# First projections of a hybrid attention and retention layer: Strassen's seven products of halves, in two passes over the input

## Chip, cores and metric

One NeuronCore of a Trainium2 chip runs the whole layer. The metric is the device time of one execution in microseconds (us), the lower the better. All data is float32. TensorE multiplies in the float32r form, and the kernel splits each operand into a high part (rounded to float32r) and a low part (what is left), so that one product is three matmuls: high x high, high x low, low x high.

## What is computed

The layer has 4096 tokens of width 1024. Cut to what matters here:

```
h = rms_norm(x, norm_gain)                  # x * rsqrt(mean(x*x) + 1e-6) * gain
proj = h @ w_in                             # 1024 -> 3584 columns
qa, ka, va, ga, qr, kr, vr, gr = split(proj, 512, 512, 512, 512, 256, 256, 512, 512)
attn = dilated_attention(rope(qa), rope(ka), va)       # 8 heads x 64, three (window, dilation) branches
ret  = retention(rotate(qr), rotate(kr), vr)           # 4 heads, keys 64, values 128
mixed = concat(silu(ga) * attn, silu(gr) * ret * ret_gain)
out = rms_norm(x + mixed @ w_out, final_gain)
```

The first stage of the kernel, `phase1`, computes five of these projections: qa and ka (1024 columns), the retention's qr and kr (512 together), and the attention's va (512). It rotates q, k and r by position and stores all of them in DRAM.

## The kernel before

There are three stages. `phase1` makes the first projections. `phase2` runs the attention heads, with the retention between their pieces as filler. `phase3` computes the gates and the output projection. In every stage the program order of each engine's instructions is written out by hand (`manual_schedule` with `ORDERED`: TensorE, ScalarE = ACT, VectorE = DVE, GpSimd = POOL, SyncE = SP). An engine takes its instructions in that order, so one that waits holds up all behind it on its engine.

`phase1` before the change goes through 8 blocks of 512 tokens. The input comes transposed, with channels on the partitions: 8 tiles of 128 channels x 512 tokens per block. `make_h` (L163 to L175) treats each tile: ACT squares it (L168) and rounds the high part (L169), DVE subtracts for the low part (L170), and POOL adds the square to a running sum (L172). The tile that takes the square has one buffer, so the next square waits for that addition. The RMS scale comes at the end of a block: `root` sums over partitions on TensorE (L188), takes the power -0.5 on POOL (L199) and builds a diagonal (L201); `along_free` turns it into a row over tokens (L209, L211). The cosine and sine tables are multiplied by that row on POOL (`scaled`, L217), so q, k and r are scaled while they are rotated.

A block has 12 weight-stationary banks (four each of q, k, r; weights 128 x 128 stationary, 512 tokens moving) and four banks of v, in which 128 tokens are stationary and 512 weight columns move. Each bank takes 8 channel tiles x 3 matmuls, so a block is 16 x 24 = 384 matmuls of 512 columns. `rotate` (L235 to L260) reads two finished PSUM banks A and B: four multiplications by tables with an operand in PSUM (L240 to L243), a subtraction and an addition (L244, L245). For q and k, ACT rounds the high part (L252 for q; L257 for k, in a permuted order) and DVE subtracts (L253, L258); SP issues the stores (L259, for r L248). `store_values` scales v on ACT (L273) and issues six stores per 128 tokens from ACT's own queue (L275, L278, L282).

All weights stay in SBUF: they are loaded and split at the start (`Split.split`, L83 and L84). After the last block the second stage begins with values of the retention, chunk by chunk (`filler`; matmuls L48 to L50 on `V`); the chunks' inputs are split in `split_h_chunk` (L432, L435).

Of the kernel before, what the change touches and what calls it, by code (L numbers as in the profile page):

```python
# [24 lines left out]
S = 4096  # L25
D = 1024
# [87 lines left out]

def phase1(tc, io, dr, right, ahead):
# [5 lines left out]
    with ExitStack() as ctx:  # L121
        wp = ctx.enter_context(tc.tile_pool(name="p1w", bufs=1))
        hp = ctx.enter_context(tc.tile_pool(name="p1h", bufs=9))
        xp = ctx.enter_context(tc.tile_pool(name="p1x", bufs=4))
        sm = ctx.enter_context(tc.tile_pool(name="p1s", bufs=2))
        tp = ctx.enter_context(tc.tile_pool(name="p1t", bufs=1))
        op = ctx.enter_context(tc.tile_pool(name="p1o", bufs=2))
        pmm = ctx.enter_context(tc.tile_pool(name="p1mm", bufs=7, space=PSUM))
        pss = ctx.enter_context(tc.tile_pool(name="p1ss", bufs=1, space=PSUM))
        ctx.enter_context(tc.manual_schedule(engines=ORDERED))  # L130

# [6 lines left out]
        qgain = wp.tile([128, KT], F32, name="qgain1")  # L138
        nc.vector.tensor_scalar(qgain, gain, -0.125, None, ALU.mult)

        W = {}
        qp = ahead["qp"] = {0: right.open("p2q")}
        wpool = ahead["wpool"] = right.open("p12w")
        for g in ("r", "k", "q", "v"):
            p = {"v": wp, "q": wpool}.get(g) or right.open(f"p1w{g}")
            i = "qkrv".index(g)
            W[g] = Split(
                nc,
                p,
                f"w1{g}",  # L150
                io["w1"][:, i * 512 : (i + 1) * 512],
                scale=qgain if g == "q" else gain,
                tag="w" if g == "q" else None,
                room=[(qp[0], "q00"), (qp[0], "q10")] if g == "r" else None,
            )

        def load_xt(b, k):
            x = xp.tile([128, BLK], F32, tag="x", name="xt1")
            nc.sync.dma_start(x, io["xT"][k * 128 : (k + 1) * 128, b * BLK : (b + 1) * BLK])
            return x  # L160
# [3 lines left out]
        def make_h(b, k, raw):  # L164

            h = hp.tile([128, 2, BLK], F32R, tag="h", name="h1")
            sq = tp.tile([128, BLK], F32, tag="sq" if k else "acc", name="sq1")
            nc.scalar.activation(sq, raw, AF.Square)  # L168
            nc.scalar.activation(h[:, 0, :], raw, AF.Copy)  # L169
            nc.vector.tensor_tensor(h[:, 1, :], raw, h[:, 0, :].bitcast(F32), ALU.subtract)  # L170
            if k:
                nc.gpsimd.tensor_tensor(sums[b], sums[b], sq, ALU.add)  # L172
            else:
                sums[b] = sq
            return h  # L175

        def load_tables(b, n):
            tab = tp.tile([128, 2, BLK], F32, tag=f"tab{n}", name=f"tab{n}1")
            for i, nm in enumerate((f"cos{n}", f"sin{n}")):
                nc.sync.dma_start(tab[:, i, :], io[nm][:, b * BLK : (b + 1) * BLK].unsqueeze(0).broadcast_to([4, 32, BLK]))  # L180
            return tab
# [33 lines left out]
        def scaled(tab, rb):  # L215
            for i in range(2):
                nc.gpsimd.tensor_tensor(tab[:, i, :], tab[:, i, :], rb, ALU.mult)  # L217

        def products(g, i, hs, p, ks=range(KT)):

            for k in ks:
                mm3(
                    nc,
                    p,
                    [(*W[g].at(k, slice(i * 128, i * 128 + 128)), hs[k][:, 0, :], hs[k][:, 1, :])],
                    k == 0,
                    k == KT - 1,
                )

        def bank():  # L230
            return pmm.tile([128, BLK], F32, tag="mm", name="mm1")

        def rotate(b, kind, idx, A, B, tab):
            cols = slice(b * BLK, (b + 1) * BLK)
            cos, sin = tab[:, 0, :], tab[:, 1, :]  # L235
# [3 lines left out]
            t4 = tp.tile([128, BLK], F32, tag="u", name="t4_1")  # L239
            nc.vector.tensor_tensor(o1, A, cos, ALU.mult)  # L240
            nc.vector.tensor_tensor(t4, A, sin, ALU.mult)
            nc.vector.tensor_tensor(t2, B, sin, ALU.mult)
            nc.vector.tensor_tensor(o2, B, cos, ALU.mult)  # L243
            nc.vector.tensor_tensor(o1, o1, t2, ALU.subtract)  # L244
            nc.vector.tensor_tensor(o2, o2, t4, ALU.add)  # L245
            for part, o in enumerate((o1, o2)):
                if kind == "r":
                    nc.sync.dma_start(dr["r"][idx, :, part, :, cols], o)  # L248
                    continue
                hl = op.tile([128, 2, BLK], F32R, tag="hl", name="hl1")  # L250
                if kind == "q":
                    nc.scalar.activation(hl[:, 0, :], o, AF.Copy)  # L252
# [10 lines left out]
        def values(b, i, k, hs, p):  # L263
            cs = slice(i * 128, (i + 1) * 128)
            mm3(nc, p, [(hs[k][:, 0, cs], hs[k][:, 1, cs], *W["v"].at(k, slice(0, 512)))], k == 0, k == KT - 1)

# [27 lines left out]
        for _ in range(4):  # L294
            load_first()
        for k in range(KT):
            W["q"].split(k)
            hcur.append(make_h(0, k, xts[k]))
            if len(xts) < KT:
                load_first()  # L300
# [1161 lines left out]
```

## Time and profile before

| | |
|---|---|
| median of 3 runs | 2414.75 us (2413.61 to 2418.51) |
| the profiled execution | 2416.7 us, span 2414.9 us |
| mean granted clock of TensorE | 0.988 |
| busy: TensorE (PE) | 2342.5 us, 97% |
| busy: its weight loads (PEld) | 1986.1 us, 82% |
| busy: DVE, ACT, POOL | 1485.8, 990.0, 725.0 us |
| DMA | 362.59 MB, mean 150 GB/s |

How to read the lines below. The page's busy list has, for each engine, the busy time, its share of the span and the count of instructions. A window line has, for a stretch of time in us, its length, then busy time and count for PE, PEld, DVE, ACT and POOL (or for the one engine asked for), then the mean granted clock of TensorE (1.00 is full), the busy share of the DMA engines, and GB/s. A timeline line has start, duration, engine, source line, operation, output <- inputs, shape, count, and in brackets the idle time before it and what ended it. A group line has the same for all instructions of a line and form: busy us and mean ns of one, then the idle time before them with its releasers. A busy PE is not PE at its peak, since the ends of matmuls are modelled: the distance between starts, or the count in a window, gives the rate.

### The profile page before, as it was taken

To read this page: it belongs to the slowest core of one execution; us is meant where nothing else is said; L and a number is where in the kernel's file an instruction comes from. 1 tells how busy PE (TensorE), PEld (TensorE's weight loads), DVE (VectorE), ACT (ScalarE), POOL (GpSimd) and SP (SyncE) were. 2 spreads that over 40 slices of the span, in tenths; PEclk is the share of its full clock that TensorE was granted. 3 is DMA by queue.
4 is the path that set the end of the run, shared out by engine and by line. 5 is a ranking of instruction groups with operands and counts; after the bars stand their busy time and mean duration, and the time that the engine had idled before them with its cause. 6 is when DMAs were issued, how large, how long until landed. Compare 5 with 4: busy or idle time off the path is not lost. (4 is left out here: it accounts for less than half of the span.)

```text
span 2414.9 us, 41800 instructions
## 1 busy us (share of the span) xinstructions
PE 2342.5 (97%) x14568; PEld 1986.1 (82%) x14568; DVE 1485.8 (62%) x3923; ACT 990.0 (41%) x2865; POOL 725.0 (30%) x765
## 2 busy tenths in 40 slices
PE   7999999999997999999999999998899999999998
PEld 5778888888885888888888887877789899999997
DVE  5643543543534878787887879786665565665654
ACT  4322222222211666666666666667222222222221
POOL 5312112112112535353544535455221121121110
PEclk9999999999998999999999999999999999999999
DMA  6343343343356766758586765746575656656553
GB/s 192 130 145 107 133 144 107 133 144 111 129 147 202 165 163 139 181 131 189 131 180 148 169 156 131 176 125 196 143 182 154 145 171 152 145 168 154 142 153 92
DMA packets 404259, 362.59 MB, mean 150 GB/s; under 512 B 191848, under 2 KB 334824, under 8 KB 398928
## 3 DMA queue, kind: packets, MB, share of 16 engines
q1 hardware_dynamic: 389408, 332.91, 52.6%
q10 hardware_dynamic: 14112, 25.43, 3.4%
q8 instruction: 115, 1.88, 0.3%
q0 software_dynamic: 528, 1.58, 0.2%
q14 instruction: 96, 0.79, 0.1%
HBM read 241.18 MB, written 118.64 MB: 149 GB/s over the span
## 5 line engine op out<-in xcount | busy, mean ns | idle before, releaser
L688 DVE CUSTOM_DVE_ANT_0 S<-S,mask 128x256 f32<-128x256 f32 (+1 forms) x768 | 308.4, 402 | 156.7 <-PE S L667 123.5
L695 ACT ACTIVATE P<-S,nm 128x256 f32<-128x256 f32 (+1 forms) x768 | 337.2, 449 | 46.9 <-DVE nm L688 43.9
L50 PE MATMUL g<-h,wg 128*128 128x256 f32 x1024 | 290.6, 284 | 0.0
L704 PE MATMUL T<-ident,P 128*128 128x128 f32 x1368 | 213.3, 274 | 0.0
L49 PE MATMUL po<-wo,m 128*128 128x512 f32 x512 | 200.6, 392 | 0.0
L50 PEld LDWEIGHTS g<-h,wg 128*128 128x128 f32 x1024 | 197.1, 192 | 0.0
L737 PE MATMUL O<-pt,v 128*64 128x128 f32 (+1 forms) x1968 | 195.8, 325 | 0.0
L667 PE MATMUL S<-kk,qc 128*128 128x256 f32 x1024 | 186.9, 306 | 6.8 <-issue 2.8
L48 PE MATMUL po<-wohi,m 128*128 128x512 f32 x448 | 178.9, 399 | 6.9 <-ACT m L40 5.4
L1251 POOL TENSOR_TENSOR rs<-v,mhalf 128x1 f32<-128x1 f32 x32 | 17.5, 547 | 547.0 <-DVE v L1249 384.9
L667 PEld LDWEIGHTS S<-kk,qc 128*128 128x128 f32 x1024 | 150.0, 191 | 34.7 <-issue 17.5
L50 PE MATMUL po<-wohi,m 128*128 128x512 f32 x448 | 176.9, 396 | 0.2 <-DVE m L41 0.2
L172 POOL TENSOR_TENSOR sq<-sq,sq 128x512 f32<-128x512 f32 x56 | 76.3, 1362 | 331.4 <-ACT sq L168 331.4
L435 POOL TENSOR_TENSOR hc<-hr,hc 128x512 fp32r<-128x512 f32 x64 | 85.9, 1343 | 289.3 <-ACT hc L434 149.6
L737 PEld LDWEIGHTS O<-pt,v 128*64 128x64 f32 x1968 | 121.2, 137 | 60.3 <-issue 31.2
L704 PEld LDWEIGHTS T<-ident,P 128*128 128x128 f32 x1368 | 163.8, 141 | 0.2 <-ACT wg0hi L87 0.2
L695 ACT ACTIVATION_READ_ACCUMULATOR P<-S,nm 128x1 f32 x768 | 157.5, 205 | 0.0
L48 PE MATMUL g<-h,wg1hi 128*128 128x256 f32 x512 | 145.9, 286 | 4.6 <-ACT e L1190 4.5
L40 ACT ACTIVATE m<-e 128x256 fp32r<-128x256 f32 x128 | 53.1, 417 | 234.5 <-DVE e L1197 137.8
L49 PE MATMUL g<-h,wg1hi 128*128 128x256 f32 x512 | 146.9, 287 | 0.9 <-DVE h L483 0.7
L48 PE MATMUL g<-h,wg0hi 128*128 128x256 f32 x512 | 144.8, 283 | 1.8 <-ACT e L1190 1.8
L49 PE MATMUL g<-h,wg0hi 128*128 128x256 f32 x512 | 144.9, 283 | 0.0
(212 smaller groups left out, 6120.7 us busy)
## 6 DMA issues: line engine op xcount, KB each, us to landing
q<-dr_q SPq DMA_DIRECT2D x128, 256.0 KB
hr<-in_xT_dram SPq DMA_DIRECT2D x64, 512.0 KB
wb<-dr_w SPq DMA_DIRECT2D x128, 192.0 KB
o<-dr_o SPq DMA_DIRECT2D x192, 128.0 KB
v<-dr_v SPq DMA_DIRECT2D x94, 256.0 KB
xt<-in_xT_dram SPq DMA_DIRECT2D x64, 256.0 KB
dr_q<-hl SPq DMA_DIRECT2D x32, 512.0 KB
dr_k<-hl SPq DMA_DIRECT2D x32, 512.0 KB
```

Source lines behind the costliest of these rows:

```text
L40: nc.scalar.activation(dst[:, 0], src, AF.Copy)
L48: nc.tensor.matmul(out, wh, xh, start=first and i == 0, stop=False)
L49: nc.tensor.matmul(out, wh, xl, start=False, stop=False)
L50: nc.tensor.matmul(out, wl, xh, start=False, stop=last and i == n - 1)
L172: nc.gpsimd.tensor_tensor(sums[b], sums[b], sq, ALU.add)
L435: nc.gpsimd.tensor_tensor(hc[:, :, 1, :], src, hc[:, :, 0, :].bitcast(F32), ALU.subtract)
L667: nc.tensor.matmul(s[:, j * 256 : (j + 1) * 256], qq[h, t, half][:, off : off + 128] if br == 0 else it["q"][:, t, i, :], rhs, start=(j == ...
L688: nc.vector.tensor_tensor_reduce(sv, sv, mask[:, it["br"], c0:256], 1.0, BIG, ALU.add, ALU.min, accum_out=nm[:, col : col + 1])
L695: nc.scalar.activation(it["P", i // 2][:, i % 2, c0:256], sv, AF.Exp, bias=nm[:, col : col + 1], scale=-1.0, accum_out=den[:, col : col + 1])
L704: nc.tensor.transpose(t[:, j * 128 : (j + 1) * 128], it["P", bank][:, j // 2, j % 2 * 128 : j % 2 * 128 + 128], ident)
L737: nc.tensor.matmul(o[64 * bank : 64 * bank + 64, c0 : c0 + 128 * m], vt[h, br, idx // 8][:, idx % 8, :], it["pt"][:, a : a + m, :].rearran ...
L1251: nc.gpsimd.tensor_tensor(rs, v, mhalf, ALU.pow)
```

## The change

The multiplication X W is cut into halves in three directions: the 1024 channels (`part` 0 and 1, four tiles each), a block's 512 tokens (`half`, 256 each), and the columns of the weights (two halves). Eight products of halves are replaced by seven (Winograd's form of Strassen's method): `P1`, `P2`, `P6`, `P5`, `P7`, `P3`, `P4`, in this order. P6, P5, P7 and P4 take sums of halves of x (POOL, `sum_t`); P6, P5, P7 and P3 sums or differences of halves of the weights, made once per pass. Results are collected in PSUM banks x, y and z (`SUMS`); copies of unfinished banks are taken by ACT (`snapshot`), and added back by DVE (`join`).

There are two passes over the input. In the first (q = 0 to 7) the weight halves make the attention's q (bank 0) and k (bank 1); in the second (q = 8 to 15) the retention's q and k together (bank 0), and v (bank 1; tokens are stationary there). Each product has one step per bank, so a block of a pass has 14 steps (`STEPS`), each of 24 matmuls of 256 columns. Input is loaded in both passes; the RMS row of the second is read from DRAM. Everything else is put on steps: `at(step, fn)` places work behind that step's matmuls, in the order in which it was entered, first that of an earlier block, then the inputs of the next.

v is now stored from SP's queue. q's factor -0.125 is applied when it is stored. The weights of the second pass are prepared around step 112 into tiles that the first pass leaves (loads of 2 MB, sums on DVE and POOL, splits on ACT with DVE or POOL), and its P4 weights a little later. At the start the loads of weights (128-column pieces, 512 bytes) and of half blocks of x alternate. At the end k, q, the retention's value weights and the first x chunk of the second stage are loaded and split in the last ten steps. The second stage's pools are opened at the beginning. The other stages are unchanged.

The core of the diff, removed lines left out:

```
+PRODUCTS = ("P1", "P2", "P6", "P5", "P7", "P3", "P4")
+SUMS = {"P1": "x", "P2": "y", "P6": "x", "P5": "z", "P7": "x", "P3": "z", "P4": "x"}
+HALF = BLK // 2
+STEPS = 2 * NP
...
+        rawp = pool("p1x", 3)
+        hp = pool("p1h", 3)
+        dp = pool("p1d", 2)
+        tp = pool("p1t", 1)
+        op = pool("p1o", 2)
+        mp = pool("p1m", 7)
+        pyz = pool("p1y", 2, space=PSUM)
+        pss = pool("p1ss", 1, space=PSUM)
+        pz = pool("p1z", 2, space=PSUM)
+        px = pool("p1px", 3, space=PSUM)
...
+        def split_x(q, prod, engine=None, each=False):
+            t = xs[q, prod] = hp.tile([128, 2, 4, HALF], F32R, tag="h", name="h1")
+            src = source(q, prod)
+            for ks in [slice(k, k + 1) for k in range(4)] if each else [slice(0, 4)]:
+                nc.scalar.activation(t[:, 0, ks, :], src[:, ks, :], AF.Copy)
+                (engine or nc.vector).tensor_tensor(t[:, 1, ks, :], src[:, ks, :], f32(t[:, 0, ks, :]), ALU.subtract)
...
+        def square(q, j):
+            sq = tp.tile([128, BLK], F32, tag="sq" if j else "acc", name="sq1")
+            nc.scalar.activation(sq, xraw[q, j // 4][:, j % 4, :], AF.Square)
+            if j:
+                nc.gpsimd.tensor_tensor(sums[q], sums[q], sq, ALU.add)
...
+        def snapshot(q, s, bank, name, half):
+            t = M[q, name, bank] = mp.tile([128, 512], F32, tag="m", name="m1")
+            p = banks[q, s, bank]
...
+                nc.scalar.activation(t, p, AF.Copy)
...
+        def join(q, s, bank, name, half, part):
+            t, p = M[q, name, bank], banks[q, s, bank]
...
+                nc.vector.tensor_tensor(t, p, t, ALU.add)
...
+        def rotate(q, bank, half):
+            if half == 0:
+                A, B = M.pop((q, "m1", bank)), banks.pop((q, "x", bank))
+            else:
+                A, B = M.pop((q, "u2", bank)), M.pop((q, "m5", bank))
...
+            nc.vector.tensor_tensor(two(t2), two(B), sin, ALU.mult)
+            nc.vector.tensor_tensor(two(o2), two(B), cos, ALU.mult)
+            nc.vector.tensor_tensor(two(o1), two(A), cos, ALU.mult)
+            nc.vector.tensor_tensor(two(A), two(A), sin, ALU.mult)
             nc.vector.tensor_tensor(o1, o1, t2, ALU.subtract)
+            nc.vector.tensor_tensor(o2, o2, A, ALU.add)
...
+        def inputs(q):
+            s = STEPS * q
+            at(s - 14, load_x, q, 0)
+            at(s - 8, load_x, q, 1)
+            if q < NBLK:
+                for j in range(4):
+                    at(s - 7 + j, square, q, j)
+                    at(s - 3 + j // 2, square, q, 4 + j)
+            at(s - 4, sum_t, q, 1)
+            at(s - 4, split_x, q, "P1")
+            at(s - 2, split_x, q, "P2")
+            at(s - 2, sum_t, q, 2)
+        for q in range(NB2):
+            s = STEPS * q
+            first, last = q % NBLK == 0, q % NBLK == NBLK - 1
+            if q:
+                inputs(q)
+            at(s, split_x, q, "P6")
+            at(s + 2, split_x, q, "P5", nc.gpsimd)
+            at(s + 3, sum_t, q, 3)
+            at(s + 4, split_x, q, "P7")
+            at(s + 6, split_x, q, "P3", nc.gpsimd if q >= NBLK or last else None)
+            at(s + 7, sum_t, q, 4)
+            at(s + 8, split_x, q, "P4", nc.gpsimd if last else None)
+            if q < NBLK:
+                at(s + (2 if q else 6), make_root, q)
+                at(s + (5 if q else 8), make_rb, q)
+            else:
+                at(s + 5, load_rb, q)
+            at(s + 7, load_tables, q)
+            at(s + 9, scale_tables, q)
+            for bank in range(2):
+                at(s + 1 + 2 * bank, snapshot, q, "x", bank, "m1", 0)
+                at(s + 6 + bank, snapshot, q, "x", bank, "u2", 1)
+                at(s + 8 + bank, snapshot, q, "z", bank, "m5", 1)
+                at(s + 4 + bank, join, q, "y", bank, "m1", 0, 0)
+                at(s + 9 + bank, join, q, "x", bank, "m5", 1, 1)
+                at(s + 11 + bank, join, q, "z", bank, "u2", 1, 0)
+            if q < NBLK:
+                order = ((11, 0, 1), (13, 0, 0), (15, 1, 0), (17, 1, 1))
+            else:
+                order = ((11, 0, 1), (12, 1, 1), (13, 0, 0), (14, 1, 0))
+            for n, bank, half in order:
+                at(s + n, last_sum, q, bank, half)
...
+        for step in range(STEPS * NB2 + 5):
+            q, i = divmod(step, STEPS)
+            prod, bank = PRODUCTS[i // 2] if q < NB2 else None, i % 2
+            if step in start:
+                start[step]()
+            if q < NB2 and step >= 4:
+                product(W[q // NBLK], q, prod, bank, units=(0, 1))
+            for fn, args, kw in todo.pop(step, []):
+                fn(*args, **kw)
```

`last_sum` calls `rotate`, or in the second pass scales and stores v. Each tuple of `order` is a step, a bank and a half: (15, 1, 0) and (17, 1, 1) fall on steps 1 and 3 of the next block.

More of the change, by code (lines that the diff above doesn't have):

```diff
@@ L137, in phase1 @@
         make_identity(nc, ident)
[L138 to L160, printed above, removed]
-        sums = {}
[L164 to L172, printed above, removed]
-            else:
-                sums[b] = sq
-            return h
@@ L213, in along_free @@
             return rb
-        def scaled(tab, rb):
-            for i in range(2):
[L217 to L231, printed above, removed]
@@ new lines, in phase1, with is_v, rcol @@
+        M = {}
+        def is_v(q, bank):
+            return q >= NBLK and bank == 1
+        def rcol(q, half, u):
+            n = 4 * (q % NBLK) + 2 * half + u
+            return rs[:, n : n + 1]
+        def snapshot(q, s, bank, name, half):
+            t = M[q, name, bank] = mp.tile([128, 512], F32, tag="m", name="m1")
+            p = banks[q, s, bank]
+            if is_v(q, bank):
+                for u in range(2):
+                    us = slice(256 * u, 256 * u + 256)
+                    nc.scalar.activation(t[:, us], p[:, us], AF.Copy, scale=rcol(q, half, u))
+            else:
+                nc.scalar.activation(t, p, AF.Copy)
@@ L309, in phase1 @@
-        diag = root(0)
-        for k in range(KT):
-            W["k"].split(k)
-        rb = None
-        def make_room(gi):
-            if gi == 1:
-                ahead["qq"] = {(0, i, 0): load_q(nc, qp, dr, 0, i, 0) for i in range(2)}
-            if gi == 3:
-                ahead["w2"] = Split(nc, wpool, "w2", io["w2"], scale=gain, tag="w")
-                ahead["w2"].load(xp.tile([128, BLK], F32, tag="x", name="raw1"))
-        GROUPS = [("q", 0), ("q", 1), ("k", 0), ("k", 1), ("r", 0), ("r", 1)]
@@ new lines, in phase1, with w2_load, w2_split, first_k @@
+        for i in range(2):
+            for k in (2 * i, 2 * i + 1):
+                at(s + 3 + 2 * i, split_p4, k)
+                at(s + 5 + 2 * i, split_p4_end, k)
+        def w2_load():
+            ahead["w2"] = Split(nc, wpool, "w2", io["w2"], scale=gain, tag="w")
+            ahead["w2"].load(mp.tile([128, 512], F32, tag="m", name="raw1"))
+        def w2_split(ks):
+            for k in ks:
+                ahead["w2"].split(k)
+        def first_k():
+            ahead["kk"] = load_k(nc, kka, dr, 0)
@@ new lines, in phase1 @@
+        for k in range(4):
+            load_x(0, 0, (k, H2))
+            load_w(0, Bb[k], 1, 4 + k)
+            load_w(0, Ba[k], 1, k)
+            load_x(0, 1, (k, H2))
+        for prod, t, part in (("P1", Aa, 0), ("P2", Ab, 1)):
+            h = xs[0, prod] = hp.tile([128, 2, 4, HALF], F32R, tag="h", name="h1")
+            for k in range(4):
+                split_w(0, prod, t, part, ks=[k])
+                src = source(0, prod)[:, k, :]
+                nc.scalar.activation(h[:, 0, k, :], src, AF.Copy)
+                nc.vector.tensor_tensor(h[:, 1, k, :], src, f32(h[:, 0, k, :]), ALU.subtract)
+                for bank in range(2):
+                    product(W[0], 0, prod, bank, [k])
```

444 lines of the change are left out of this document (305 added, 139 removed).

## Prediction

> **What bounds the kernel now.** I read the page first, its busy list and its slices; then the windows of 100 us; then the timeline of single engines in one block of the first stage.
>
> ```profile
> PE 2342.5 (97%) x14568; PEld 1986.1 (82%) x14568; DVE 1485.8 (62%) x3923; ACT 990.0 (41%) x2865; POOL 725.0 (30%) x765
> ```
>
> ```profile
> 0.00:100.00 100.00, 84.38 (x336) 65.41 (x337) 60.25 (x75) 40.76 (x64) 46.04 (x37) 0.97 0.53 170
> 300.00:400.00 100.00, 100.00 (x437) 81.39 (x437) 40.28 (x55) 22.19 (x33) 18.24 (x15) 1.00 0.38 125
> 700.00:800.00 100.00, 82.93 (x400) 68.22 (x400) 49.27 (x103) 22.15 (x46) 23.16 (x28) 0.91 0.68 191
> ```
>
> TensorE is never idle in the middle of the stage: 437 matmuls of 512 columns in 100 us, 0.229 us each, at the full clock, while DVE is busy for 40 of 100 us and POOL for 18. So this stage is bound by TensorE, and matmul columns saved there are time saved, as long as the others keep up. The stage begins and ends less well filled.
>
> **The matmuls.** The timeline of TensorE gives the price of a 256-column product, from the gates of the last stage, and the end of the first stage:
>
> ```profile
> 1903.23 0.28 PE L48 MATMUL g<-h,wg1hi 128*128 128x256 f32 x1
> ...
> 1906.09 0.40 PE L48 MATMUL po<-wohi,m 128*128 128x512 f32 x1
> ```
>
> ```profile
> 756.31 0.39 PE L50 MATMUL mm<-w1vhi,h 128*128 128x512 f32 x1
> ```
>
> Twenty-four 256-column matmuls lie between the first two rows: 2.86 us, 0.119 us each, 4% more per column than at 512. Removed are 8 blocks x 384 = 3072 matmuls of 512 columns (703 us at 0.229). Added are 16 half passes x 14 steps x 24 = 5376 of 256 (641 us); a step is 2.86 us and a block of 14 steps 40.05 us. The matmuls alone give back 62 us. [...]
>
> **What else a block of the first pass needs.** Rows of one block before, from the timelines of DVE, POOL and ACT:
>
> ```profile
> 376.44 0.69 DVE L170 TENSOR_TENSOR h<-xt,h 128x512 fp32r<-128x512 f32 x1 [0.91 <-ACT h L169]
> 386.18 1.36 DVE L170 TENSOR_TENSOR h<-xt,h 128x512 fp32r<-128x512 f32 x1 [3.60 <-ACT h L169]
> 416.77 0.69 DVE L240 TENSOR_TENSOR o<-mm,tabA 128x512 f32<-128x512 f32 x1 [15.40 <-DMA dr_rs<-rb]
> 419.83 0.69 DVE L244 TENSOR_TENSOR o<-o,t 128x512 f32<-128x512 f32 x1
> 420.43 0.69 DVE L245 TENSOR_TENSOR o<-o,t 128x512 f32<-128x512 f32 x1
> 476.64 1.36 DVE L170 TENSOR_TENSOR h<-xt,h 128x512 fp32r<-128x512 f32 x1 [3.58 <-ACT h L169]
> ```
>
> ```profile
> 385.70 1.28 POOL L172 TENSOR_TENSOR sq<-sq,sq 128x512 f32<-128x512 f32 x1 [4.68 <-ACT sq L168]
> 415.44 2.55 POOL L217 TENSOR_TENSOR tabA<-tabA,rb 128x512 f32<-128x512 f32 x2 [11.86 <-ACT rb L211]
> ```
>
> ```profile
> 387.01 0.63 ACT L168 ACTIVATE sq<-xt 128x512 f32<-128x512 f32 x1 [0.87 <-POOL sq L172]
> 389.05 0.63 ACT L168 ACTIVATE sq<-xt 128x512 f32<-128x512 f32 x1 [0.88 <-POOL sq L172]
> ```
>
> ```profile
> L258 DVE TENSOR_TENSOR hl<-o,hl 128x512 fp32r<-128x512 f32 x24 | 28.1, 1227 | 9.0 <-ACT hl L257 9.0
> L169 ACT ACTIVATE h<-xt 128x512 fp32r<-128x512 f32 x53 | 33.0, 622 | 137.0 <-PE mm L50 137.0
> L257 ACT ACTIVATE hl<-o 128x512 fp32r<-128x512 f32 x24 | 27.4, 1255 | 78.3 <-DVE o L244 78.3
> L273 ACT ACTIVATE vo<-mm,rs_all 128x512 f32<-128x512 f32 x28 | 19.2, 687 | 99.4 <-DMA dr_v<-vo 89.9 <-issue 9.3
> L172 POOL TENSOR_TENSOR sq<-sq,sq 128x512 f32<-128x512 f32 x47 | 62.5, 1329 | 309.8 <-ACT sq L168 309.8
> L201 POOL TENSOR_TENSOR diag<-ident,rs_all 128x512 f32<-128x512 f32 x7 | 7.3, 1040 | 0.6
> ```
>
> The block was 476.64 - 386.18 = 90.46 us long, 2.6 more than its 384 matmuls. DVE operations follow each other by 0.60 us. The one at 386.18, which reads two SBUF tiles, ran beside POOL's addition until 386.98 and ended 0.56 us after it: it waited for POOL's whole instruction. The one at 416.77, with a PSUM operand, ran inside two POOL multiplications at no loss. So a DVE operation with two SBUF inputs and a POOL operation take turns, about 0.54 us for one and 1.16 for the other. And a square waits until POOL has added the one before (one buffer): one every 2.03 us, ACT's queue standing behind it.
>
> In the new first pass a block has 36 such DVE units of 512 elements (six splits of x, 12; four rotations, 20; the remainders of q, 4), 19.4 us, and four strided remainders of k at about 1.05, 4.2 us; POOL has 20 units (four half sums and one split at two each, seven additions, two tables, the diagonal), 23 us. Together 47 us against 40: POOL no longer hides.
>
> **The chain through one block.** Order on each queue is written out, so I follow it from t = 0, the end of step 10 (first bank of P3), when the first z bank can be joined. R01 is the rotation of q's second half, R00 its first, R10 and R11 are k's.
> - DVE: join 0.7; R01's six operations to 4.4, ACT's high parts to 5.1, remainders to 5.9.
> - ACT then has four squares ahead of P2's split: 5.1 + 3 x 2.03 + 0.63 = 11.8; its high part (1024 elements, between 0.62 and 1.24; 1.05) 12.9; DVE waits for the last addition, then the remainder: 14.3. R00 and the next rotations are queued behind it.
> - R00: two PSUM operands, 15.5, which frees the x bank that step 15 needs (due at 11.4); then behind POOL's half sum, 16.6; the rest 20.3; P6's split 21.9.
> - R10: six operations 25.6, then ACT and DVE in turn at 1.25 and 1.2 to 28.8. The copy of P1 out of x bank 0 stands behind R10 on ACT, at 28.3; step 18 overwrites that bank and waits.
> - R11: its six operations all read SBUF. P5's split (2.4), the diagonal (1.0) and two half sums (2.4 each) come to POOL just then, and each gets in between two of them: less what overlaps, 7.1 us. Without them R11's results, ACT's two high parts and the copy of x bank 1 (0.69) end at 35.2; with them at 42.3. Step 19 needs that copy; it was due at 8 x 2.86 = 22.9.
> - From step 19 to step 25 (the next t = 0) TensorE has six steps, 17.2 us, and 0.4 for the scale row. DVE, ACT and POOL catch up there.
>
> After such an idle time the clock is lower, as the windows around one of 3.5 us show (PE busy, clock, DMA):
>
> ```profile
> 54.00:56.00 2.00, 0.77 (x4) 1.00 0.00 1
> 56.00:58.00 2.00, 0.00 (x0) 0.89 0.00 0
> 58.00:60.00 2.00, 1.75 (x4) 0.50 0.00 0
> 60.00:62.00 2.00, 2.00 (x6) 0.50 0.00 0
> 62.00:64.00 2.00, 2.00 (x7) 0.50 0.50 182
> 64.00:66.00 2.00, 2.00 (x9) 0.91 0.91 342
> ```
>
> From 58.25 on 8 matmuls are missing, 1.8 us. A first-pass block is then 42.3 + 17.2 + 0.4 + 1.8 = 61.7 us (54.7 without POOL's four; 42.6 if nothing waits).
>
> **Second pass, start, change of weights, exit.** Other rows that these use:
>
> ```profile
> 20.00:30.00 10.00, 10.00 (x45) 1.00 0.97 299
> ```
>
> ```profile
> 14.13 0.74 DVE L84 SCALAR_TENSOR_TENSOR w1q<-w1q,qgain,w1qhi 128x512 fp32r<-128x512 f32 x1
> 370.02 0.69 DVE L240 TENSOR_TENSOR o<-mm,tabR 128x512 f32<-128x512 f32 x1 [5.65 <-DMA dr_r<-o]
> 394.75 3.27 ACTq L282 DMA_DIRECT2D dr_v<-vo  x4
> ```
>
> ```profile
> PE V L48 <- DVE vch L1037: 16.5, 1, 16.5
> ```
>
> - Second pass: no squares, no remainders, two rotations; DVE and POOL together stay under 30 us, so TensorE sets 40.05. R00 writes the tile whose store takes 5.65 us: bank free at 11.9 for 11.4, so 40.5. The v stores go to SP's queue: 24 issues at 0.82 us, 20 of 40 us, hidden; uncovered they would delay the next x.
> - Start: before the third product all of 6.3 MB of x and weights must land. At 299 GB/s that is 21 us; for pieces of 512 B no row stands, at half the rate it is 42; I take 30, so 32 from the start. POOL then has 14 us (difference, two half sums, split, weights of P5) before P5, 14.2 of squares before P3's split, 3.5 of split, one step: t = 0 of block 0 at 66 (57 to 78).
> - Change of weights: eight groups of four 0.74 us operations on DVE, twelve on POOL, around the end of pass one, but no squares: a block of 66 (54 to 77).
> - Exit: the second chunk's values product (its input split behind k's last store and load) kept TensorE waiting for 16.5 us. Now q and k are long in DRAM; the last rotations still stand before that chunk on DVE: 10 us gained (0 to 16.5).
>
> **Sum.** 66 + 7 x 61.7 + 66 + 7 x 40.5 + 3 steps 8.6 = 856 us for the stage, against 756.7: +99, less 10 at the exit: +89. The profiled execution took 2416.7 us (span 2414.9), 2 above the median of the three runs. Forecast 2506 us.
>
> **Rivals.**
> - *POOL's four miss R11* (its work falls into DVE's gaps): blocks of 54.7, change 59: stage 800, 2449 us. For: POOL rests between its bursts; against: P5's split is released right at R11.
> - *Faster, port alone*: queues never wait in order, only turns between DVE and POOL count: blocks of 47, change 51, stage 738, 2388 us. This decides wherever a block stays under 50.5 us, the break-even of the sum. [...] Against: P2's split behind the squares.
> - *Faster, TensorE bound throughout*: blocks of 42.6, stage 696, 2346 us. For: DVE and POOL at 40% and 18% now; against: the 47 us.
> - *The change doesn't do what it says*: weight loads, twice as many per column, set the pace:
>
> ```profile
> L50 PEld LDWEIGHTS g<-h,wg 128*128 128x128 f32 x1024 | 197.1, 192 | 0.0
> ```
>
> 5376 x 0.192 = 1032 us, about 2720 in all. Against: the gates keep 0.119 with a load for each.
>
> **How the numbers follow.** Forecast 0.53, the first rival 0.20, the port 0.11, TensorE 0.12, weight loads 0.02; 0.02 falls within 0.2% (5 us, what a measurement of this kernel can tell from no change). Faster 0.23, same 0.02, slower 0.75. The forecast's own range is 2465 to 2550 (start +-11, change +-11, exit +-8, blocks +-4 each). The range for 8 in 10 takes in the first rival and the port's price and leaves out TensorE, weight loads and the tail above: 2385 to 2550.
>
> **What would show it.** In the profile after: the first pass at about 62 us a block, TensorE idle before P6's second bank, released by ACT's copy of an x bank, and before P1's second bank, released by a DVE rotation; DVE operations on SBUF of 1 to 3 us beside POOL; squares 2 us apart; the clock under 1 in each such block; the second pass at 40 to 41 us and the clock at 1. Wrong, if TensorE has no idle time over 2 us in a middle block of the first pass, or waits there for a DMA, or if 24 matmuls take more than 2.9 us.

## The result, and the profile after

The changed kernel took 2689.03 us (median of four runs, 2679.33 to 2691.53), the kernel before 2416.63 beside it: a ratio of 1.1121, 95% interval 1.1089 to 1.1152. The forecast was 2506 us with a range to 2550. The profiled execution has a span of 2685.8 us.

The page's busy list after the change:

```profile
PE 2347.0 (87%) x16872; PEld 2116.3 (79%) x16872; DVE 1734.0 (65%) x4129; ACT 1117.9 (42%) x3039; POOL 991.5 (37%) x860
```

TensorE's busy time is what it was (2342.5 before); the time came as idle time. Two windows of 100 us, the first now in the first pass, the second in the second pass (busy time of PE, PEld, DVE, ACT, POOL, then clock, DMA share, GB/s):

```profile
300.00:400.00 100.00, 80.14 (x592) 78.30 (x591) 68.42 (x71) 36.77 (x50) 50.36 (x27) 0.88 0.38 127
700.00:800.00 100.00, 75.97 (x597) 75.63 (x596) 44.29 (x55) 17.56 (x24) 30.55 (x14) 0.86 0.39 125
```

The second window is the surprise: no square and no remainder of q or k is left there, DVE and POOL are idle more than half the time, and TensorE is idle for a quarter. TensorE's timeline names the waits (the bracket: idle time before the instruction and what ended it):

```profile
44.77 0.58 PE L407 MATMUL x<-h,w1q 128*128 128x256 f32 x1 [24.08 <-ACT m L428]
...
110.56 0.76 PE L407 MATMUL x<-h,w1wh 128*128 128x256 f32 x2 [9.60 <-DVE o L484]
...
295.00 0.77 PE L407 MATMUL x<-h,w1wh 128*128 128x256 f32 x2 [8.37 <-DVE o L484]
315.92 0.80 PE L407 MATMUL x<-h,w1q 128*128 128x256 f32 x2 [5.63 <-ACT m L428]
356.72 0.76 PE L407 MATMUL x<-h,w1wh 128*128 128x256 f32 x2 [8.65 <-DVE o L484]
...
729.83 5.07 PE L407 MATMUL x<-w1kk,h 128*128 128x256 f32 x24 [13.29 <-DVE o L484]
782.85 5.46 PE L407 MATMUL x<-w1kk,h 128*128 128x256 f32 x24 [10.73 <-DVE o L484]
```

The wait on L484, the second multiply of the rotation of half 0, stands once in each block and is always at step 15 (P1's second bank of the next block), so its release marks the blocks. Cut at these marks, with the prediction's own terms brought to the same marks (81.5 is its 66 + 15.5; the second pass's mark lies 11.9 behind its t = 0):

| stretch | predicted | after | best variant (below) |
|---|---|---|---|
| start to the first release of step 15 | 81.5 | 110.6 | 101.6 |
| six blocks of the first pass | 370.2 | 369.0 | 346.7 |
| last block of it and change of weights | 124.1 | 139.7 | 140.6 |
| six blocks of the second pass | 243.0 | 328.3 | 249.6 |
| to the end of the last product | 37.2 | 40.8 | 42.6 |
| all that follows | 1648.2 | 1697.5 | 1681.4 |
| span | 2504.2 | 2685.8 | 2562.5 |

The miss of 181.6 us is 85.3 in the second pass, 49.3 behind the stage, 29.1 in the start, 15.6 in the change, 3.6 at the end and -1.2 in the first pass.

**The first pass** runs in the order that the prediction wrote down. DVE's and ACT's timelines of one block:

```profile
340.31 2.29 DVE L483 TENSOR_TENSOR t<-m,tab 128x512 f32<-128x512 f32 x1
...
353.93 1.45 DVE L320 TENSOR_TENSOR h<-xt,h 128x1024 fp32r<-128x1024 f32 x1 [6.20 <-ACT h L319]
...
355.90 0.68 DVE L484 TENSOR_TENSOR o<-x,tab 128x512 f32<-128x512 f32 x1
...
371.64 2.72 DVE L486 TENSOR_TENSOR m<-m,tab 128x512 f32<-128x512 f32 x1
```

```profile
345.17 1.23 ACT L496 ACTIVATE hl<-o 128x512 fp32r<-128x512 f32 x2 [6.89 <-DVE o L487]
346.31 0.62 ACT L327 ACTIVATE sq<-xt 128x512 f32<-128x512 f32 x1
348.32 0.63 ACT L327 ACTIVATE sq<-xt 128x512 f32<-128x512 f32 x1 [1.39 <-POOL sq L329]
350.32 0.63 ACT L327 ACTIVATE sq<-xt 128x512 f32<-128x512 f32 x1 [1.37 <-POOL sq L329]
352.32 0.63 ACT L327 ACTIVATE sq<-xt 128x512 f32<-128x512 f32 x1 [1.37 <-POOL sq L329]
352.86 1.04 ACT L319 ACTIVATE h<-xt 128x1024 fp32r<-128x1024 f32 x1
```

R01 on DVE from 340.31; its high parts on ACT; four squares, 2.0 us apart; P2's split on ACT, then on DVE; then R00's two multiplies, whose second one, at 355.90, releases TensorE at 356.72. The row at 371.64 belongs to R11, beside POOL's work.

**The second pass** has another chain. SP's queue (issue times), then POOL, then DVE, in one block:

```profile
723.78 2.35 SPq L492 DMA_DIRECT2D dr_r<-o  x4
...
749.74 3.67 SPq L464 DMA_DIRECT2D dr_v<-vo  x4
753.52 0.38 SPq L282 DMA_DIRECT2D xt<-in_xT_dram  x1
754.00 0.45 SPq L369 DMA_DIRECT2D rb<-dr_rs  x1
754.56 0.37 SPq L282 DMA_DIRECT2D xt<-in_xT_dram  x1
754.98 0.61 SPq L375 DMA_DIRECT2D tab<-in_cosR_dram  x1
755.64 0.80 SPq L375 DMA_DIRECT2D tab<-in_sinR_dram  x1
776.83 2.35 SPq L492 DMA_DIRECT2D dr_r<-o  x4
```

```profile
765.44 1.29 POOL L379 TENSOR_TENSOR tab<-tab,rb 128x512 f32<-128x512 f32 x1 [13.17 <-DMA tab<-in_cosR_dram]
767.94 1.29 POOL L379 TENSOR_TENSOR tab<-tab,rb 128x512 f32<-128x512 f32 x1 [1.21 <-DMA tab<-in_sinR_dram]
769.19 2.38 POOL L302 TENSOR_TENSOR d<-xt 128x1024 f32<-128x1024 f32 x1
```

```profile
769.26 2.85 DVE L483 TENSOR_TENSOR t<-m,tab 128x512 f32<-128x512 f32 x1 [5.50 <-POOL tab L379]
772.05 2.82 DVE L484 TENSOR_TENSOR o<-m,tab 128x512 f32<-128x512 f32 x1
...
782.01 0.69 DVE L484 TENSOR_TENSOR o<-x,tab 128x512 f32<-128x512 f32 x1 [2.09 <-DMA dr_r<-o]
```

The queue sends the stores of one block (from 723.78 to 753.4), only then this block's tables, which POOL can scale at 765.44; R01 starts at 769.26, its first two multiplies take turns with POOL's half sums; the next r stores go out at 776.83, the v stores behind them, and the next tables behind those. It is a loop with SP's queue in it: from one block's r stores to the next it is 53.1 us (723.78 to 776.83), and 54.7 in the mean of six. The first r store waits for R01; the 31 stores behind it then follow each other almost without a gap, and issuing the 32 takes 28.7 of these 29.6 us (24 of v 23.9, eight of r 4.9).

### The profile page after: what moved, and what is told of

The parts are those of the page before. It is cut to its first block, busy times and chain, and to the rows that moved or that the text cites. A ratio compares the mean times of both kernels' runs of the same rounds, so it can differ in the third digit from the quotient of the medians.

```text
span 2685.8 us, 47219 instructions
## 1 busy us (share of the span) xinstructions
PE 2347.0 (87%) x16872; PEld 2116.3 (79%) x16872; DVE 1734.0 (65%) x4129; ACT 1117.9 (42%) x3039; POOL 991.5 (37%) x860
## 4 chain that ended last, share of the span: by engine, by line
PE 57%; DMA 14%; DVE 13%; SPq 4%; issue 4%; ACT 4%; POOL 4%; DVEq 0%; ACTq 0%; POOLq 0%
PE S L987 8%; PE O L1057 6%; PE T L1024 5%; PE po L48 4%; PE po L50 4%; PE po L49 4%; PE g L49 4%; PE g L50 4%; PE g L48 4%; PE x L407 3%; DMA tab<-in_cosR_dram 3%; PE V L48 2%; DMA tab<-in_sinA_dram 2%; PE V L50 2%; DMA dr_v<-vo 2%
## 5 line engine op out<-in xcount | busy, mean ns | idle before, releaser
L407 PE MATMUL x<-h,w1q 128*128 128x256 f32 x832 | 181.1, 316 | 68.3 <-ACT m L428 63.2
L407 PEld LDWEIGHTS x<-h,w1q 128*128 128x128 f32 x832 | 150.6, 222 | 71.7 <-ACT m L428 65.6
L319 ACT ACTIVATE h<-d 128x1024 fp32r<-128x1024 f32 x64 | 67.7, 1058 | 253.6 <-POOL d L302 147.8
L407 PE MATMUL x<-h,w1wh 128*128 128x256 f32 x384 | 89.7, 333 | 74.0 <-DVE o L484 60.5
L1510 ACT ACTIVATE e<-g 128x256 f32<-128x256 f32 x128 | 48.2, 379 | 250.9 <-PE g L50 232.1
L320 DVE TENSOR_TENSOR h<-d,h 128x1024 fp32r<-128x1024 f32 x46 | 70.2, 1526 | 125.1 <-ACT h L319 121.8
```

The source lines that it names most:

```text
L319: nc.scalar.activation(t[:, 0, ks, :], src[:, ks, :], AF.Copy)
L320: (engine or nc.vector).tensor_tensor(t[:, 1, ks, :], src[:, ks, :], f32(t[:, 0, ks, :]), ALU.subtract)
L407: nc.tensor.matmul(o, l, r, start=first and j == 0, stop=last and j == 2, skip_group_check=True)
```

## Experiments

A block time is the mean distance, over four to six blocks, between waits at the same step in that kernel's own trace (step 15's; where that is gone, another product's). "The fourfold kernel" and "best variant" are the ones named so below. The theories: 1, the order on SP's queue holds the second pass's loads back; 2, the transfers themselves are slow; 3, one chain through ACT, DVE and POOL sets the first pass; 4, the sum of what these engines do in order and in turns sets it ("port" in the prediction and the expectations is a name for the turns of DVE and POOL; the traces show turns, as at 386.18 in the kernel before, 1.36 us for 0.69, and not what lies behind them). The time of the kernel before in the same jobs was 2411 to 2417 us. A time with neither a range nor a ratio is one execution.

### Second pass

**Tables and RMS row from ACT's queue.**

```
- nc.sync.dma_start(tab[:, i, :], ...)      + nc.scalar.dma_start(tab[:, i, :], ...)
- nc.sync.dma_start(rb, ...)                + nc.scalar.dma_start(rb, ...)
```

> The changed kernel with the issues of the tables and of the RMS row (second pass) moved from SP's queue to ACT's; all else as it is. Theory 1, order on SP's queue: in the second pass the tables are issued behind 24 v stores and two loads of x, and the r stores that SP takes next wait for the rotation that needs these tables, so the block is the sum of both, 56.6 us. Off that queue the second pass falls to 40 to 43 us a block, the wait at the exit of the stage falls too, and the whole is 120 to 150 us shorter: 2540 to 2570 us. Theory 2, the transfers themselves: with 3 MB of v stores and 1 MB of x per block in flight the tables land late from any queue: second pass 53 to 57 us, whole 2670 to 2695. First pass 61 to 62 us a block by both.

2684.42 us (2681.03 to 2688.35), blocks of 54.1 us. The wait of the rotation for its tables nearly went (5.1 us in six blocks, 42.2 before), but the splits now waited for x, which had stayed on SP's queue behind the stores. So the tables alone are not it, and theories 1 and 2 are both still possible.

**The v stores on ACT's queue instead.** `nc.sync` to `nc.scalar` in the three lines of `store_values`.

> The changed kernel with the v stores back on ACT's queue, as before the change; tables stay on SP's. Theory 1 (order on SP's queue): SP is free, tables come in time; ACT issues 24 stores in about 24 us of a block of 40 and stands before the copies of the x banks there, so 42 to 48 us a block in the second pass, whole 2560 to 2620. Theory 2 (the transfers themselves): no better than 53 us a block. First pass unchanged at 61 to 62 us.

2795.53 us, blocks of 69.4; theory 1's 42 to 48 missed. The waits of ACT from 640 to 990 us (in total, how often, the longest):

```profile
ACT h L319 <- DMA dr_v<-vo: 258.5, 11, 28.8
```

ACT stood behind the stores for up to 28.8 us at a time and the splits with it: the stores held ACT's queue here, as they had held SP's (28.7 us of issues a block).

**One v store in place of four for branch 1.**

```
- for r in range(4): ... nc.sync.dma_start(dr["v"][1, r0 : r0 + 32]..., vf[r:128:4, u, :])
+ nc.sync.dma_start(v1[4 * b + i], vf[:, u, :])
```

> Branch 1's values are stored by one plain DMA of 128 rows for each chunk instead of four of 32 rows with a stride, so 12 v stores a block in place of 24; rows of that branch land in another order (the bytes are the same). In the changed kernel the four took 3.7 to 5.9 us of SP's queue for each chunk, 19 us a block; the other v stores of the same size took 0.57 to 0.86 each. Theory 1, the order on SP's queue: x, rb and both tables are issued some 16 us earlier, the second pass's blocks fall from 54.7 to 41 to 45 us, total 2590 to 2620. Theory 2, the transfers themselves (as many bytes as before): blocks stay at 53 to 56, total 2675 to 2695. First pass unchanged at 61.5 by both.

2717.84 us, ratio to before 1.1257 (1.1229 to 1.1285), blocks of 58.6: both theories missed, it became slower. SP's queue:

```profile
750.59 9.15 SPq L491 DMA_DIRECT2D dr_r<-o  x4
...
765.92 2.53 SPq L282 DMA_DIRECT2D xt<-in_xT_dram  x1
768.55 2.88 SPq L369 DMA_DIRECT2D rb<-dr_rs  x1
```

Twelve issues fewer, but the four r stores now took 9.15 us to issue and the loads 2.5 to 2.9 each, against 2.35, 0.38 and 0.45 in the rows above. So an issue has no fixed price, and counting issues at one, as my sum did, is wrong. What sets the price, and why these stores held up what came behind them more than four small ones did, was not tried.

**The second pass's loads of x, row and tables from POOL's queue.** `nc.gpsimd` in the three load lines for q >= 8.

> Second pass only: the loads of x, of the RMS row and of both tables are issued from POOL, which was busy 18 of 54 us there; SP's queue keeps nothing but the 32 stores a block, in the order they had. Nothing left out. Theory 1, the order on SP's queue: the loads no longer stand behind stores that wait for rotations, blocks fall from 54.7 to 42 to 47 us, total 2595 to 2635 (a few us held back for what issuing costs POOL, which no trace here shows). Theory 2, the transfers: 53 to 56 us, total 2675 to 2695. First pass unchanged.

2658.8 us, 1.1014 (1.0988 to 1.104), blocks of 49.9: a third of the gap to 40.5 closed; the forecast of theory 1 (42 to 47) missed as well. (In this kernel the untouched first pass had blocks of 61.4 to 64.5; its mean over the kernels that leave it alone is 61.4 to 63.3. So a single difference of 1 to 2 us there shows nothing by itself.)

**The rotation of half 0 from a copy of its bank by ACT.**

```
+ B = mp.tile(...); nc.scalar.activation(B, banks.pop((q, "x", bank)), AF.Copy)
```

> The rotation of half 0 reads a copy of its product's bank that ACT makes at the same step, so that PSUM comes free at the copy and not at DVE's second multiply; nothing left out. First pass: the copy stands on ACT behind the four squares and P2's split, so it gains the 1.5 to 2 us from that split's remainder on DVE to the second multiply, and no more: 58 to 61 us a block. Second pass: if the bound is the loop over SP's queue (tables are issued behind the v stores of the block before, which wait for its rotations, which wait for its tables), TensorE is ahead but the loop keeps its time: 53 to 55. If the bound is only the late release of PSUM: 42 to 46.

2705.7 us. Second pass 54.3: freeing PSUM earlier changes nothing while the loop over SP's queue stands, as theory 1 said. First pass 65, not 58 to 61: the copies stand in ACT's order and delay what is behind them.

**The fourfold kernel**: loads from POOL, value tiles of half 1 apart, and for the first pass the two reorderings of the next part together.

```
- vfs[q, half] = op.tile([128, 2, 512], F32, tag="hl", ...)
+ half 1: two tiles of tags "acc" and "sq"
```

> Nothing left out. Four edits: snapshots of P1 first on ACT and P2's split and half sum 2 ahead of the last four squares (both for the first pass; alone they gave 61.2 and 59.9 us a block); loads of x, RMS row and tables from POOL in the second pass; and the value tiles of half 1 in two tiles that only the first pass uses, so that a value tile is not written again while its stores are under way (with the loads on POOL, DVE's write of it stood 6.4 to 8.8 us a block). Theory 3, one loop from step 15 over eleven steps, the last P3 bank, the rotation of half 1, four squares, P2's split and the first rotation's two reads: the two edits of the first pass take 5.5 us (squares) and 5.6 us (copy of P1) out of the same loop, and only both together show it: 50 to 54 us a block. Theory 4, the totals of three engines: 58 to 61. Second pass: if the tile's stores are what is late next, 43 to 46 us a block where the loads on POOL alone gave 49.9; if it is the sum of transfers, 49 to 51. Total by theory 3 with late stores 2540 to 2580; by the others 2640 to 2660.

2622.98 us, 1.0862 (1.084 to 1.0885); second pass 49.4, so the value tiles were not it. What was late is in its POOL and DVE timelines:

```profile
826.48 2.55 POOL L379 TENSOR_TENSOR tab<-tab,rb 128x512 f32<-128x512 f32 x2 [8.71 <-DMA tab<-in_cosR_dram]
```

```profile
829.06 2.87 DVE L487 TENSOR_TENSOR t<-m,tab 128x512 f32<-128x512 f32 x1 [4.32 <-POOL tab L379]
831.85 2.88 DVE L488 TENSOR_TENSOR o<-m,tab 128x512 f32<-128x512 f32 x1
...
842.61 0.69 DVE L488 TENSOR_TENSOR o<-x,tab 128x512 f32<-128x512 f32 x1 [2.82 <-DMA dr_r<-o]
```

The tables were asked for too late in the program (step 7), and the tile of the multiply that frees the bank was still being stored.

**Row and tables asked for at steps 2 and 3**, on top of the fourfold kernel:

```
- at(s + 5, load_rb, q)      + at(s + 2, load_rb, q)
- at(s + 7, load_tables, q)  + at(s + (7 if q < NBLK else 3), load_tables, q)
```

> The fourfold kernel with only the earlier request of row and tables; nothing left out. If table and store wait stand in a row on the same path, this alone gives the table's 4.3 us and perhaps the port's turns: second pass 43.5 to 46. If the path goes over the store's wait alone: 48 to 49.5. First pass unchanged at 57 to 59.

2587.38 us, second pass 44.2: as expected, tables and DVE's turns 5.2 us.

**The best variant**: this, the second multiply of half 0 into an `m` tile, and the first weights' sums operation by operation.

> On top of the fourfold kernel (57.9 and 49.5 us a block), nothing left out: the second pass's RMS row and tables are asked for at steps 2 and 3 instead of 5 and 7; the rotation of half 0 writes its second multiply, the one that frees the PSUM bank, into a tile that no store holds (it stood 2.8 us for the stores of the rotation before it); and the first weights' sums are issued operation by operation over the four tiles instead of tile by tile. If the second pass's wait of 8 us at step 15 is these two in a row (tables 4.3, stores 2.8, and DVE's two multiplies at 2.87 instead of 0.68 beside POOL's sums): 42 to 45 us a block, near the 40.5 of my sum. If TensorE waits for something else by then: 47 to 50. Start: P6's wait of 23 us ends 5 to 7 us earlier. Exit: the next stage's first chunk no longer stands behind a rotation that waits for tables, another 5 to 10. Total 2550 to 2580, against 2600 to 2620.

2559.84 us, 1.0591 (1.0569 to 1.0614); second pass 41.6, three middle blocks 40.06 to 40.07, the others 42.1 and twice 43.6. One of the three (columns as above):

```profile
671.16:711.22 40.06, 40.06 (x338) 40.06 (x337) 25.00 (x29) 11.18 (x16) 20.85 (x13) 1.00 0.56 180
```

TensorE is busy throughout, at full clock, with a DMA share of 0.56: the same bytes pass in 40 us (7.2 MB, 180 GB/s for 40.06 us; from 729.83 to 782.85 in the changed kernel 135 GB/s, 7.2 MB as well), so theory 2 falls. This is the 40.05 of the sum. The tables' own transfer is a small part of the gain: in the fourfold kernel POOL, waiting for them, starts 10.1 us after the first issue from its own queue (816.34 to 826.48), in the changed kernel 10.5 and 12.3 us after the issues from SP's (754.98 to 765.44, 755.64 to 767.94).

**The same with the loads back on SP's queue** (and the start as in the changed kernel).

> The kernel that came to 41.6 us a block in the second pass (early request of row and tables, a free tile for the second multiply, value tiles of half 1 apart, the order of the first pass), but with the loads of x, row and tables back on SP's queue and the start as in the changed kernel; nothing left out. Rows and tables are asked for at steps 2 and 3 in the order of the program, which on SP's queue is still behind the 32 stores of the block before. If that order is what the second pass lacked: 50 to 55 us a block again. If the early request and the free tile were enough by themselves: 40 to 44. First pass 57 to 59 by both.

2650.41 us, second pass 53.7. The queue:

```profile
719.53 3.37 SPq L468 DMA_DIRECT2D dr_v<-vo  x4
723.01 0.39 SPq L282 DMA_DIRECT2D xt<-in_xT_dram  x1
...
723.99 0.61 SPq L375 DMA_DIRECT2D tab<-in_cosR_dram  x1
```

Asked for earlier or not, the loads leave behind the last store. That one edit is worth 12 us a block here; theory 1 stands, with two more waits in a row behind it.

### First pass

**Snapshots of P1 first in ACT's order.** `todo.setdefault(step, []).insert(0, ...)` for them.

> The changed kernel with the copies of P1 out of the x banks entered ahead of everything else of their step, so ACT makes them before it rounds the rotations of k. Theory 3, the chain of the prediction: the wait of 5.6 us before step 19 goes, and P7's split, behind the rotation on DVE, is late next at step 22: 53 to 55 us a block in the first pass, whole about 45 to 55 us shorter. Theory 4, shared port alone: DVE and POOL have the same turns to take, and the time comes back at the next wait: 59 to 62 us a block.

2678.78 us, blocks of 61.2, as theory 4 said. The wait of step 19 went, the one of step 15 grew from 8.4 to between 10.4 and 12.2, and one of 3.3 came at step 22.

**P2's split and half sum 2 ahead of the last four squares.**

```
- at(s - 3 + j // 2, square, q, 4 + j)   + at(s - 2 + j // 2, square, q, 4 + j), behind split and sum
```

> The changed kernel with P2's split and the second half sum ahead of the squares, and the last four squares one step later each. Theory 3 (chain): the 5.5 us in which DVE waits for P2's high part behind four squares go, P6's split then stands behind two squares: the wait before step 15 falls from 8.4 to 3 to 5 us, a first-pass block from 61.5 to 56 to 58 us, whole 25 to 40 us shorter. Theory 4 (port alone): the additions now meet R00, and the block stays at 60 to 62.

2668.86 us, blocks of 59.9: the wait as theory 3 said, the block just under theory 4's 60. Step 15's wait fell to 2.9, two waits on ACT's copies grew to 2.7 and 5.6 to 8.4.

**Half sums 3 and 4 left out** from block 1 on.

> From block 1 on the half sums 3 and 4 are left out (products P7 and P4 take sums 1 and 2 again), so POOL does 6.5 us less in every block of both passes. They lie at steps 3 and 7, ahead of the waits of the first pass. Theory 3, the one chain of my prediction (square, sum and split of the next block behind each other at steps 10 to 15): the first pass stays at 60 to 62 us a block. Theory 4, the sum of work that DVE, POOL and ACT do in order and in turns on their tiles (DVE 42.3, POOL 31 of 61.3 us): POOL's turns against DVE's operations with two inputs in SBUF fall away, and the block takes 54 to 58. Second pass: nothing by theory 1, which has its loads late.

2668.62 us, 61.1 a block: POOL's 6.5 us less work at these two places gave nothing, as theory 3 said.

**The remainders of q and k left out.**

> The remainders of q and k (eight DVE operations a block, 28.1 us in three blocks, 9.4 us a block) are left out; the store reads the head twice, so bytes and issues stay. Theory 4: DVE is the longest of the three engines beside TensorE, its order ends step 15's wait, and the first pass falls by about the 9.4 us, to 51 to 54 us a block. Theory 3 (the chain runs over POOL and ACT, DVE's rotations are in it only up to the o tile): 59 to 62. Second pass unchanged at 54 to 56 (it makes no remainders of q and k).

2657.38 us, 58.3 a block: 3.2 of the 9.4 us that DVE no longer worked. Neither theory's figure.

**Both reorderings together** (the fourfold kernel): 57.9 a block, where theory 3 had said 50 to 54. Its DVE timeline shows where the rest went, in R01:

```profile
322.26 1.76 DVE L487 TENSOR_TENSOR t<-m,tab 128x512 f32<-128x512 f32 x1
323.94 2.88 DVE L488 TENSOR_TENSOR o<-m,tab 128x512 f32<-128x512 f32 x1
326.75 1.77 DVE L489 TENSOR_TENSOR o<-m,tab 128x512 f32<-128x512 f32 x1
328.55 2.78 DVE L490 TENSOR_TENSOR m<-m,tab 128x512 f32<-128x512 f32 x1
```

Three of the same four take 0.68 to 0.69 us in the changed kernel, where POOL rests (342.53 to 344.53, POOL idle from 342.05 to 347.00). Here POOL's half sums and additions, now earlier, run just beside them (POOL busy throughout from 321 to 330), and R01 needs 10.4 us (322.26 to 332.64); in the changed kernel it took 5.5 (340.31 to 345.84).

**With the copy of the rotation's bank as well.**

> The edits of the fourfold kernel and the copy of the rotation's bank together; nothing left out. By theory 3 with the late stores: first pass 48 to 53, second pass 41 to 44, total 2520 to 2570. If ACT's order takes up what DVE gives: as without the copy, within 1% of it.

2626.11 us, 1.087 (1.0849 to 1.0891), first pass 59.7, second 47.7: within 0.2% of the fourfold kernel. The totals agree because two changes cancel: the first pass lost 1.8 us a block, with ACT's order taking up what DVE gives and more, and the second gained 1.7.

**The best variant without remainders** (and without its edit at the start).

> The same without the change at the start, and with the remainders of q and k left out in the first pass (eight DVE operations, some 10 us a block; the store reads the head twice). First pass: if DVE's order is what ends each of its waits, now that ACT's order is mended, 48 to 51 us a block where it gave 57.9; if POOL's and ACT's, 54 to 58 (without the mended order the same omission gave 58.0 in place of 61.5). Second pass as in the kernel beside it, 42 to 45.

2525.09 us, first pass 51.8 against 57.8, second 41.0: near the figure for DVE's order, 48 to 51. One block of it:

```profile
209.28:260.94 51.66, 44.35 (x347) 43.08 (x347) 37.24 (x38) 21.69 (x31) 28.53 (x16) 0.96 0.40 133
```

With ACT's order mended, DVE's share counts for more than before (6.0 us instead of 3.2 for the same omission; by the spread of the untouched first pass the 3.2 could be up to 5). So in the changed kernel two things lay side by side: the chain of theory 3 (ACT's order), and DVE's own order with its turns; taking out one alone shows little.

## Why the prediction was wrong, and where it was right

**The step that failed** is this one: "The v stores go to SP's queue: 24 issues at 0.82 us, 20 of 40 us, hidden; uncovered they would delay the next x." They were uncovered. I asked how long the issues take, and not what stands between them: stores wait for rotations, rotations for tables, and the tables stand behind the stores of the block before. With the stores and the tables' loads on one queue in order, the times add up (stores 723.78 to 753.4, tables' landing and scaling to 769.2, R01 to 776.8), 53 us a turn. The run with the loads back on SP's queue shows it as a cause: 53.7 against 41.6 us. What stands ahead has to be counted with an issue: the five loads' own issues take 2.6 us a block, the 32 stores ahead of them 28.7, which my sum put at 20 without the r stores. In the best variant the stores take no less (the last 23 of one block's 32, from 714.70 to 742.42, 25.8 us of issues; the same 23 of the changed kernel's block about 20.8) and are hidden, since no load stands behind them. So the size of the term was a small part of the error; the loop was the greater.

**"Bank free at 11.9 for 11.4"** covered the store of the r tile alone (5.65 us in the row of before). The tables' request at step 7 and DVE's turns with POOL's half sums (two multiplies of 2.8 us each that take 0.68 alone) were missing: 5.2 us together, as the early request showed, and the tile's wait the next 2.6. "DVE and POOL together stay under 30 us, so TensorE sets 40.05" was too low in its sum (25.0 and 20.9 us in the best variant's block above, 45.9 together) and right in the bound, since the two mostly run side by side: the best variant reaches 40.07. A total under the bound says nothing about when the work may start.

**Second pass, start, change, exit**, each said as a lump:
- Start, 29.1 us more. P6 waited 24.08 us for ACT (44.77 in the first fence), which stood in order behind a chain of sums and splits for one weight tile after the other. Issuing these by operation gave 3.7 us to the first release (105.3 to 101.6, the fourfold kernel against the best variant), the reorderings 5.2. The 20 us left were not taken apart. The 30 us in my sum for x and weights lay between the full rate and half of it for pieces of 512 B; no run shows the half: from 5 to 30 us the DMA engines moved 254 to 311 GB/s in every 5 us.
- Change, 15.6 more: no edit was aimed at it, and it stayed at 140.6 in the best variant. Its cause is open.
- Exit, forecast 10 better, came 39.3 worse (1697.5 against 1658.2). TensorE, DVE and SP after the last product:

```profile
1008.54 0.76 PE L48 MATMUL V<-w2hi,hc 128*128 128x512 f32 x1 [20.29 <-DVE hc L752]
...
1030.96 0.55 PE L987 MATMUL S<-kk,q 128*128 128x256 f32 x1 [8.53 <-DMA q<-dr_q]
```

```profile
1002.73 0.69 DVE L483 TENSOR_TENSOR t<-m,tab 128x512 f32<-128x512 f32 x1 [12.17 <-POOL tab L379]
...
1007.98 0.76 DVE L752 CAST hc<-hr 128x512 fp32r<-128x512 f32 x2
```

```profile
983.03 0.61 SPq L375 DMA_DIRECT2D tab<-in_cosR_dram  x1
...
1018.94 3.74 SPq L464 DMA_DIRECT2D dr_v<-vo  x4
1022.73 3.96 SPq L860 DMA_DIRECT2D q<-dr_q  x8
```

The last rotations did stand before the chunk, as I wrote, but they waited for tables, and the load of q stood behind v stores: the same queue. With the second pass's loads on POOL's queue and nothing else changed, the first wait was 9.6 us for 20.3, the one for q 9.6, and all that follows took 1678.7 us, 18.8 less. The fourfold kernel (1680.8) and the best variant (waits of 10.0 and 13.3, 1681.4) are no better, so the early request of the tables gave nothing more here. The order behind the load of q was argued from the trace, not tried, and the rest of the 39.3 was not taken apart.

**The first pass** was right in its total, 61.5 for 61.7, and in its waits: P1's second bank on DVE's multiply, P6's second bank on ACT's copy, squares 2 us apart, the clock under 1 (0.86). Its terms were not all right. One block:

```profile
233.61:295.00 61.39, 47.45 (x346) 46.46 (x347) 42.34 (x46) 21.77 (x30) 31.02 (x17) 0.86 0.34 112
```

The idle time was 13.9 us a block where mine sum to 19.4; RMS matmuls with their row and the lower clock cost 7.4 (47.45 us of busy time for 40.05) where I had 2.2. These errors cancelled, so that the total came within 0.2 us was luck. And the chain was not the only limit: its two largest links, taken out together, gave 3.6 us, since DVE's turns with POOL moved to another rotation. Two terms of the chain had the wrong size. Step 15's bank came free later: TensorE started there 20.2 us after the end of step 10 (336.49 to 356.72), where mine says 15.5. The term for POOL's four operations beside R11 (7.1 us) was too large: R11's six operations took 5.9 us (369.72 to 375.57) and R10's 3.8 (362.86 to 366.67), so POOL cost 2.1 before the copy, and the two half sums come behind it; leaving them out gave 0.4 us. Step 19 began at 41.1 for 42.3.

**The product's rate** held: 40.06 us for 14 steps of 24, 2.86 a step. The saving of 62 us in matmuls is real; the best variant gets it in the second pass only, and stays 6% slower than before. The fourth rival's 2720 us lies near the measured time by chance: its mechanism, weight loads that set the pace, does not occur (14 steps of 24 matmuls in 40.06 us). The range was too narrow at its upper end because every term that could make the second pass longer than TensorE was put at nothing, its alternative named and not priced.

## What to carry to other kernels

When a queue holds loads and stores, follow the loop through it: what the store waits for, what that waits for, and whether this load stands behind the store; the loop's sum was the bound here (53.1 us a turn), not the issues' total (28.7). Give loads that the next block needs a queue without stores that wait for computing, and ask for them as early as their tile is free. Where two loops lie within a few microseconds of each other, undoing one shows little (61.2 and 59.9 us a block alone, 57.9 together, from 61.5); undo both before a theory is dropped.

## What the runs showed of the hardware that was not expected

- The time of one issue on SP's queue is not fixed: the first load of x behind the v stores took 0.38 us to issue in the changed kernel (753.52) and 2.53 and 3.17 (765.92, 822.98) in the one with a single v store for branch 1, which moves the same bytes. What sets it was not tried.
- In one block of the changed kernel (723.78 to 753.4) stores of 32 rows, a stride of four partitions apart, took 0.9 to 1.5 us each to issue; plain ones of 128 rows and four times the bytes 0.57 to 0.86 beside them.
- The cost of a wait was not proportional to its length. In one block of the fourfold kernel a wait of 4.0 us on TensorE was followed by 2.9 us at clock 0.50 and one of 3.3 by 6.1 us of it; a third stretch of 3.4 us (288.84 to 292.26) has no wait longer than 0.81 us in the 9 us ahead of it, with the eight one-column matmuls of the RMS sum right behind that short wait. The six changes of the clock there (278.60, 282.02, 288.84, 292.26, 309.30 and 316.14, worked out to about 0.03 us from the mean clock of windows of 2 to 3 us, with 1.00 and 0.50 as its two values) lie 3.42, 6.82, 3.42, 17.04 and 6.84 us apart. What sets their times was not tried.
